# Rank scatter of 128 row tiles: 15 in place of 12 tiles as row copies from HBM to HBM, and loads of one row a partition

## The chip, the cores and the metric

The kernel runs on one core of a Trainium2 chip. The metric is the device time of one execution in microseconds, median of three runs. A profile of one execution, taken by the hardware profiler, gives the durations used below.

## The reference

Each of 8 batches has 2048 scores and 2048 rows of 2560 f32 (10 KB a row). A row goes to the place that the rank of its score has in its batch:

```python
B, N, D = 8, 2048, 2560            # x: (B, N, D) f32, scores: (B, N) f32
order = np.argsort(scores, axis=1)
ranks = np.argsort(order, axis=1)
out[b_idx, ranks, :] = x
```

The 168 MB of x are read once and the 168 MB of the output written once. The only arithmetic is the counting that gives the ranks.

## The kernel before

A tile is 128 rows of one batch, so there are 16 tiles a batch and 128 in all. The table `GROUPS` joins tiles into groups: `(first row, tiles in the group m, batches whose group goes directly)`. With m = 2 a partition of a load holds two neighbouring rows of x (20 KB in one piece), and the two tiles of the group are the even and the odd rows of 256. A group and a batch that the table names as direct are in the list `DIRECT`; all others are in `BULK`. Both lists go batch by batch, and inside a batch by `ORDER`.

*Ranks.* TensorE transposes the scores into columns (`s_col`, L167) and, for each batch, spreads its 2048 scores over all partitions (L188); VectorE copies these to `s_all` (L234). For each tile VectorE counts the scores that are smaller, or equal and earlier (L257: one count for the columns from the group's first on, one for the columns before it, and one product with a triangular mask over the group's own columns for ties). It adds the counts (L283, L289) to `rank`. A bulk group's ranks are cast to integers (`rank_i`, L306). A direct group's ranks are transposed by TensorE (L299), and VectorE turns them into byte addresses in the output (`rows_i`, L219); it does so after the counts of the group that follows.

*Bulk tiles.* SP issues the first `NBUF` loads (L119) as its first work. POOL then goes through `BULK` in order: it waits until the scatters of group k - `LAG` have landed, issues the load of group k + `NBUF` - `LAG` into the buffer that came free (L119), waits for group k's load and ranks, and issues one indirect scatter a tile (L375), 128 rows of 10 KB each.

*Direct tiles.* After its loads SP goes through `DIRECT`, and ACT, which has no other work, does the same. Each copies half of the rows of a tile. A loop (`Fori`, L331) makes four passes a tile; a pass loads 16 byte addresses from `rows_i` into registers (L332) and issues 16 copies of one row, from x to the output in HBM (L343), each split over the 16 DMA engines as 640 bytes a piece. Of the 12 direct tiles each of the two engines so copies 768 rows, in 48 passes. SP waits at the end for all rows and all scatters.

POOL's transfers go through one DMA queue, SP's through a second and ACT's through a third; all three are served by the same 16 DMA engines, and each queue has a ring on every one of them.

The lines that set the split, the buffers and the lead:

```python
GROUPS = [(0, 2, (0, 1, 2, 3, 4, 5)), (256, 2, ()), (512, 2, ()), ...]
NBUF = 8
LAG = 2
G = 16
```

Of the kernel before, what the change touches and what calls it, by code (L numbers as in the profile page):

```python
# [40 lines left out]
def kernel(  # L41
# [11 lines left out]

    GROUPS = [(0, 2, (0, 1, 2, 3, 4, 5)), (256, 2, ()), (512, 2, ()), (768, 2, ()), (1024, 2, ()), (1280, 2, ()), (1536, 2, ()), (1792, 2, ())]
    ORDER = [0, 1, 2, 3, 4, 5, 6, 7]
    MMAX = max(m for _, m, _ in GROUPS)
    MDIR = max([m for _, m, direct in GROUPS if direct], default=1)
    MBULK = max(m for _, m, direct in GROUPS if len(direct) < B)  # L60
    BULK = [(b, g) for b in range(B) for g in ORDER if b not in GROUPS[g][2]]
    DIRECT = [(b, g) for b in range(B) for g in ORDER if b in GROUPS[g][2]]

    PARTS = [(0, 128)]
    NBUF = 8
    LAG = 2
    G = 16

    def first_col(g):
        return GROUPS[g][0] // P  # L70

# [14 lines left out]
    rows_i = [pool.tile([MDIR, P], I32, name=f"rows_i{i}") for i in range(len(DIRECT))]  # L86
    xb = [pool.tile([P, MBULK * D], F32, name=f"x{i}") for i in range(NBUF)]
    ps_col = psum.tile([P, 512], F32, name="ps_col")
# [11 lines left out]
    with tc.tile_critical(no_gpsimd_drain=True):  # L100
# [5 lines left out]
        s_scores = nc.alloc_semaphore("scores")  # L106
        s_first = [nc.alloc_semaphore(f"first{i}") for i in range(NBUF)]
        s_load = [nc.alloc_semaphore(f"load{i}") for i in range(NBUF)]
        s_scat = [
            [nc.alloc_semaphore(f"scat{i}_{j}") for j in range(MBULK * len(PARTS))]  # L110
            for i in range(NBUF)
        ]
        s_rows = {sp: nc.alloc_semaphore("rows_sp"), act: nc.alloc_semaphore("rows_act")}
        n_scat = [[0] * (MBULK * len(PARTS)) for _ in range(NBUF)]

        def load(line, k, sem):
            b, g = BULK[k]
            r, m, _ = GROUPS[g]
            line.eng.dma_start(  # L119
                out=xb[k % NBUF][:, :m * D],  # L120
                in_=x[b, r:r + P * m, :].rearrange("(p j) d -> p (j d)", j=m),
            ).then_inc(sem, 16)
# [106 lines left out]
        for b in range(B):  # L229
# [11 lines left out]
            dve.after(dve, t_copied)  # L241
            for g in ORDER:
                r, m, _ = GROUPS[g]
# [110 lines left out]
        def scatters_done(k):  # L354
            i = k % NBUF
            for j in range(GROUPS[BULK[k][1]][1] * len(PARTS)):
                pl.wait(s_scat[i][j], 16 * n_scat[i][j])

        for k, (b, g) in enumerate(BULK):
            i = k % NBUF  # L360
            r, m, _ = GROUPS[g]
            if k >= LAG and k + NBUF - LAG < len(BULK):
                scatters_done(k - LAG)
                load(pl, k + NBUF - LAG, s_load[(k - LAG) % NBUF])
            if k < NBUF:
# [52 lines left out]
```

## Time and profile before

| | |
|---|---|
| median of 3 runs | 819.38 us (818.96 to 819.45) |
| time of the profiled execution | 818.96 us |
| its span | 817.2 us |
| VectorE busy | 408.7 us (50%), done by about 425 us |
| POOL busy | 142.2 us (17%) |
| HBM read and written | 167.84 MB and 167.77 MB, 411 GB/s over the span |
| first loads on SP | 8 of 2560 KB |
| loads on POOL | 50 of 2560 KB |
| scatters on POOL | 116 |
| row copies | 768 on SP, 768 on ACT |

The span runs from the first to the last instruction; the time of the execution holds a little more around it. Issuing a DMA does not count as busy time of an engine, so SP and ACT have next to no busy time though their row loops run for most of the span. They are read from the timeline, where the engine is written SPq or ACTq. The busy share of the DMA is the mean over 16 DMA engines.

### The profile page before, as it was taken

Reading aid. Unit: us, or ns where it says so; the run is one execution under the profiler, and the core shown is the slowest. Engines: PE = TensorE matmul, PEld = TensorE weight load, DVE = VectorE, ACT = ScalarE, POOL = GpSimd, SP = SyncE. Lnnn points to the kernel's source line nnn. Section 1 sums busy time; section 2 is a strip of 40 time slices with the busy share of each in tenths; the row PEclk is TensorE's granted clock in tenths of the full one; section 3 lists DMA queues with packets and bytes.
Section 4 is the critical chain, followed back from the end, with each engine's and each line's share of the span. In section 5 each row is a group of like instructions: output and inputs, shape, how many; then the busy total and the mean of one; then the engine's idle time right before and its main releaser. Section 6 shows DMA issues by size and latency. Waiting matters only on the chain.

```text
span 817.2 us, 8185 instructions
## 1 busy us (share of the span) xinstructions
PE 31.5 (4%) x150; PEld 27.1 (3%) x150; DVE 408.7 (50%) x962; ACT 0.0 (0%) x1; POOL 142.2 (17%) x175
## 2 busy tenths in 40 slices
PE   3001010010100101000000000000000000000000
PEld 3001010010100101000000000000000000000000
DVE  6999999999999999999960000000000000000000
ACT  0000000000000000000000000000000000000000
POOL 0111212121212111212111111212121212150000
PEclk9555555555555555555555555555555555555555
DMA  8999999999999999999999999999999999999810
GB/s 366 417 427 426 412 426 413 425 417 419 424 417 423 410 410 376 412 420 417 415 415 406 419 417 421 410 413 415 394 407 405 410 409 423 395 414 422 361 35 8
DMA packets 74248, 320.20 MB, mean 392 GB/s; under 512 B 27368, under 2 KB 51944, under 8 KB 51944
## 3 DMA queue, kind: packets, MB, share of 16 engines
q0 software_dynamic: 23904, 283.13, 82.6%
q1 hardware_dynamic: 25744, 28.95, 10.2%
q10 hardware_dynamic: 24576, 7.91, 4.0%
q14 instruction: 23, 0.19, 0.1%
q8 instruction: 1, 0.02, 0.0%
HBM read 167.84 MB, written 167.77 MB: 411 GB/s over the span
## 4 chain that ended last, share of the span: by engine, by line
DMA 44%; DVE 40%; POOL 3%; issue 3%; PE 1%; POOLq 0%; SPq 0%
DMA out_dram<-x,rank_i 42%; DVE trash L257 35%; DMA x<-in_x_dram 2%; POOL out_dram L375 2%; DVE s_all L234 2%; DVE rank L283 1%; DVE rank L289 1%; POOL x L119 1%; DVE rank_i L306 1%; PE ps_all L188 0%; DMA s_in<-in_scores_dram 0%; PE ps_col L167 0%; DVE rows_i L219 0%; POOLq L28 0%; DVE s_col L175 0%
## 5 line engine op out<-in xcount | busy, mean ns | idle before, releaser
L257 DVE TENSOR_SCALAR_CACHE_REDUCE trash<-s_all,s_col 128x1792 bf16<-128x1792 f32 (+7 forms) x240 | 314.5, 1345 | 0.3
L375 POOL DMA_INDIRECT out_dram<-x,rank_i x116 | 112.2, 967 | 65.4 <-issue 36.7
L119 POOL DMA_DIRECT2D x<-in_x_dram x50 | 28.2, 564 | 531.2 <-DMA out_dram<-x,rank_i 353.1
L257 DVE SCALAR_TENSOR_TENSOR trash<-s_all,s_col,mask 128x256 bf16<-128x256 f32 x128 | 61.4, 480 | 0.0
L188 PE MATMUL ps_all<-ident,s_col 128*128 128x128 f32 x128 | 27.5, 404 | 275.0 <-DVE s_all L234 274.6
L188 PEld LDWEIGHTS ps_all<-ident,s_col 128*128 128x128 f32 x128 | 24.6, 215 | 276.9 <-DVE s_all L234 276.5
L234 DVE COPY s_all<-ps_all 128x512 f32<-128x512 f32 x32 | 20.2, 685 | 1.9 <-PE ps_all L188 1.6
L257 DVE DVE_READ_ACCUMULATOR trash<-s_all,s_col 128x1 f32 x240 | 19.7, 82 | 0.0
L289 DVE TENSOR_TENSOR rank<-rank,acc 128x2 f32<-128x2 f32 x64 | 10.3, 161 | 2.2
L283 DVE TENSOR_TENSOR rank<-acc,acc 128x2 f32<-128x2 f32 x64 | 10.3, 161 | 2.2
L306 DVE CAST rank_i<-rank 128x2 int32<-128x2 f32 x58 | 9.7, 167 | 1.8
L257 DVE DVE_READ_ACCUMULATOR trash<-s_all,s_col,mask 128x1 f32 x128 | 10.5, 82 | 0.0
L175 DVE COPY s_col<-ps_col 128x128 f32<-128x128 f32 x1 | 0.3, 293 | 4.7 <-PE ps_col L167 4.7
L299 PE MATMUL ps_row<-ident,rank 128*2 128x128 f32 x6 | 1.9, 322 | 15.0 <-DVE rank L289 15.0
L167 PE MATMUL ps_col<-ident,s_in 8*128 8x8 f32 x16 | 2.1, 264 | 3.8 <-DMA s_in<-in_scores_dram 3.8
L167 PEld LDWEIGHTS ps_col<-ident,s_in 8*128 8x128 f32 x16 | 2.0, 211 | 3.8 <-DMA s_in<-in_scores_dram 3.8
L219 DVE TENSOR_SCALAR rows_i<-ps_row 2x128 int32<-2x128 f32 x6 | 1.6, 272 | 0.0
L299 PEld LDWEIGHTS ps_row<-ident,rank 128*2 128x2 f32 x6 | 0.5, 80 | 17.1 <-DVE rank L289 17.1
L148 POOL TENSOR_SCALAR_AFFINE_SELECT mask<-mask 128x256 f32<-128x256 f32 x2 | 0.8, 398 | 0.0
L160 DVE MEMSET acc<- 128x128 f32 x1 | 0.2, 165 | 1.1 <-SPq L100 1.1
L131 POOL MEMSET mask<- 128x512 f32 x1 | 0.5, 525 | 0.0
L130 POOL MEMSET ident<- 128x128 f32 x1 | 0.2, 204 | 0.5 <-SPq L100 0.5
(6 smaller groups left out, 0.7 us busy)
## 6 DMA issues: line engine op xcount, KB each, us to landing
x<-in_x_dram POOLq DMA_DIRECT2D x50, 2560.0 KB, 19.3
x<-in_x_dram SPq DMA_DIRECT2D x8, 2560.0 KB, 31.4
out_dram<-in_x_dram ACTq DMA_DIRECT2D x768, 10.0 KB
out_dram<-in_x_dram SPq DMA_DIRECT2D x768, 10.0 KB
out_dram<-x,rank_i POOLq DMA_INDIRECT x116, 24.1
s_in<-in_scores_dram SPq DMA_DIRECT2D x1, 64.0 KB
```

Of the source, the lines that this page charges most:

```text
L119: line.eng.dma_start(out=xb[k % NBUF][:, :m * D], in_=x[b, r:r + P * m, :].rearrange("(p j) d -> p (j d)", j=m),).then_inc(sem, 16)
L148: nc.gpsimd.affine_select(out=part, in_=part, pattern=[[0, MMAX], [-1, P]], compare_op=OP.is_ge, fill=0.0, base=-half, channel_multiplier=1,)
L167: nc.tensor.transpose(out=ps_col[:, B * c:B * (c + 1)], in_=s_in[:, r + j:r + m * P:m], identity=ident[:B, :B],)
L188: nc.tensor.transpose(out=ps_all[:, P * c:P * (c + 1)], in_=s_col[:, c, b:b + 1].to_broadcast([P, P]), identity=ident[:],)
L219: nc.vector.tensor_scalar(out=rows_i[DIRECT.index((b, g))][:m, :], in0=ps_row[:m, :P], scalar1=float(b * N), scalar2=float(ROW), op0=OP.ad ...
L234: nc.vector.tensor_copy(out=s_all[:, 512 * q:512 * (q + 1)], in_=ps_all[:, 512 * q:512 * (q + 1)],)
L257: how.pop("do")(out=trash[i][:, :P * (hi_c - lo_c)], in0=s_all[:, P * lo_c:P * hi_c], accum_out=acc[which][:, col:col + 1], **how,)
L283: nc.vector.tensor_tensor(out=rank[:, cols], in0=acc[0][:, cols], in1=acc[1][:, cols], op=OP.add)
L289: nc.vector.tensor_tensor(out=rank[:, cols], in0=rank[:, cols], in1=acc[2][:, cols], op=OP.add)
L299: nc.tensor.transpose(out=ps_row[:m, :P], in_=rank[:, cols], identity=ident[:])
L306: nc.vector.tensor_copy(out=rank_i[:, cols], in_=rank[:, cols])
L375: nc.gpsimd.indirect_dma_start(out=out_flat, out_offset=bass.IndirectOffsetOnAxis(ap=(rank_t if lo else rank_i)[:hi - lo, col:col + 1], axis=0
```

## The change

```diff
-    GROUPS = [(0, 2, (0, 1, 2, 3, 4, 5)), (256, 2, ()), (512, 2, ()), (768, 2, ()), (1024, 2, ()), (1280, 2, ()), (1536, 2, ()), (1792, 2, ())]
-    ORDER = [0, 1, 2, 3, 4, 5, 6, 7]
+    GROUPS = [(0, 1, (0, 1, 2, 3, 4, 5, 6, 7)), (128, 1, (0, 1, 2, 3, 4, 5, 6)), (256, 1, ()), (384, 1, ()), (512, 1, ()), (640, 1, ()), (768, 1, ()), (896, 1, ()), (1024, 1, ()), (1152, 1, ()), (1280, 1, ()), (1408, 1, ()), (1536, 1, ()), (1664, 1, ()), (1792, 1, ()), (1920, 1, ())]
+    ORDER = [0, 1, 2, 3, 4, 5, 6, 7, 8, 9, 10, 11, 12, 13, 14, 15]
...
-    NBUF = 8
-    LAG = 2
+    NBUF = 15
+    LAG = 4
```

Every group is now one tile of 128 neighbouring rows. The first tile of all eight batches and the second tile of seven go directly: 15 tiles, 960 rows for each of SP and ACT. The other 113 tiles are loaded one by one, 1.31 MB each with one 10 KB row a partition, 15 of them by SP and 98 by POOL. There are 15 buffers of one tile in place of 8 of two, and POOL loads 11 tiles ahead of the one it scatters, where it was 6 pairs. The columns of the counts, the masks, the adds and the casts follow the group's size.

## The prediction

> **What bounds the kernel now.** I read the DMA part of the page first, then the stretches of the span, then the timelines of SP and ACT.
>
> ```profile
> DMA  8999999999999999999999999999999999999810
> ...
> q0 software_dynamic: 23904, 283.13, 82.6%
> q1 hardware_dynamic: 25744, 28.95, 10.2%
> q10 hardware_dynamic: 24576, 7.91, 4.0%
> ```
>
> The 16 DMA engines are full for 37 of 40 slices and nearly idle in the last two. q0 is POOL's queue (scatters and later loads), q1 is SP's, q10 ACT's. The stretches give the edge:
>
> ```profile
> 66.00:720.00 654.00, 20.13 (x87) 16.76 (x85) 351.09 (x832) 0.00 (x0) 121.56 (x147) 0.51 1.02 413
> 720.00:770.00 50.00, 0.00 (x0) 0.00 (x0) 0.00 (x0) 0.00 (x0) 12.32 (x13) 0.50 1.02 418
> 770.00:817.00 47.00, 0.00 (x0) 0.00 (x0) 0.00 (x0) 0.00 (x0) 0.00 (x0) 0.50 0.18 51
> ```
>
> The last three numbers of a line are clock, DMA share (over 1 where packets of one engine overlap) and GB/s. Until 770 us the DMA is the limit; after it the share is 0.18, and something else holds the end for 47 us. SP's timeline says what:
>
> ```profile
> 24.43 783.95 SPq L343 DMA_DIRECT2D out_dram<-in_x_dram  x768
> 80.15 624.72 SPq L343 DMA_DIRECT2D out_dram<-in_x_dram  x624
> 724.79 42.38 SPq L343 DMA_DIRECT2D out_dram<-in_x_dram  x32
> 783.38 11.68 SPq L343 DMA_DIRECT2D out_dram<-in_x_dram  x16
> 796.70 11.68 SPq L343 DMA_DIRECT2D out_dram<-in_x_dram  x16
> 24.39 53.83 ACTq L343 DMA_DIRECT2D out_dram<-in_x_dram  x64
> ```
>
> The row loops run through the whole span, and SP's last row leaves at 808.4. So the kernel ends with SP's loop, not with the scatters. (The chain of waits shows scatters and VectorE because a loop that is never idle has no wait to follow; its VectorE pieces up to 334 us are an artefact, as VectorE is then on batch 6 and POOL on about tile 50.) Three paces of a row follow. **Free**, the last two passes of 16 rows start 13.32 us apart: 0.833 us a row. **DMA full but the loop's own queue not backed up**, ACT's first 64 rows, the next pass starting at 79.8: 55.4/64 = 0.866. **Steady**, SP from 80.15 to the pass at 706.58: 626.4/624 = 1.004. A fourth, while only scatters run (724.79 to the pass at 769.98): 45.2/32 = 1.41.
>
> ```profile
> L343 SPq DMA_DIRECT2D out_dram<-in_x_dram x768: 520/529/2122, 24.4 to 807.9; - x192
> L332 SPq TENSOR_LOAD <-rows_i x48: 973/1641/3729, 23.0 to 795.5; - x48
> ```
>
> Minimum, median and maximum: an issue costs at least 520 ns, an address load at least 973 ns a pass. In the free stretch row issues start 0.741 us apart; 16 of these and about 1.46 us for load and loop make the 13.32. What is above that is blocking: a row sent too early finds the queue full (counted from issues and packets, at most about 32 rows of a queue are outstanding).
>
> **The change, part by part.**
>
> *Rows.* 12 tiles become 15, so each loop does 960 rows in place of 768, in 60 passes in place of 48. Instructions per row are unchanged. Even with no blocking ever, 960 x 0.833 = 800 us of sequencer time. This is the largest term.
>
> *Where the loops start.* The first rank is now of one column. The first count ended at 13.1, the second column's needs 3 us more, so rows_i comes near 17 instead of 22.5, and rows could start near 19 instead of 24.4. SP cannot use it: its first loads (15 of 1.31 MB, 19.7 MB, in place of 21.0) stand ahead of its rows in q1. Before, the last packet of these loads started at 65.7. In the trace a 20 KB load packet takes 761 ns (median), a 10 KB scatter packet 385, a row's share on one engine 34 + 9 (640 bytes and its semaphore). Queues alternate packet by packet, so q1 with 20 KB packets had two thirds of the rate beside q0; with 10 KB packets it has half. By 26 us (first scatter) q1 has moved (26 - 2)/0.39 = 61 of its 120 packets per engine; the other 59 at 0.39 + 0.385 + 0.04 = 0.82 us end at 74 to 76. By then SP has issued what its queue holds, about 35 rows.
>
> *Pace in the bulk.* This is the unknown. Between two packets of q0 an engine takes one of SP and one of ACT (after 770, on the engine that is still scattering, every 10 KB packet is followed by one of each), and a row is two packets, so two rounds. Before, a pair of tiles was 8 load rounds of 0.76 + 0.043 and 16 scatter rounds of 0.385 + 0.043, 13.3 us for 24 rounds or 12 rows: 1.11 us a row, measured 1.004. With 10 KB loads every round is 0.43: 0.86 a row, or 0.92 on an engine at 415 ns a packet as the last one ran. By that the queue now keeps up with the issue, whose pace under a full DMA is 0.866. Bounds: 0.833 (free) and 1.41 (the scatter stretch, where every q0 packet is 10 KB too; I take it for a property of scatters alone, as the loads' half of the time still writes no HBM). I take 0.89, midway between 0.866 and 0.92, because both limits are near; 0.866 to 1.004 go into the range.
>
> *Bulk.* Per engine, before until 770: 464 x 0.786 + 928 x 0.386 + some 1450 rows x 0.043 = 785 us of packets in 768 us. After: 904 x (0.392 + 0.386) + some 1600 x 0.043 = 772, so 755 us by the same ratio; with the slower start I take 762 for the end of the bulk. If 10 KB loads cost 0.41 instead, it is 16 us later; the loops are then slower for 16 us longer, worth 16 x (1 - 0.833/0.89) = 1 us at the end.
>
> *Edits at nothing.* VectorE: L283 and L289 64 more each (161 ns), 55 more casts (167), 9 more rows_i (272), 8 more counts, against narrower mask products (480 ns at 256 wide): at most +35 us on 409. It is done near 425 us and the last scatter issues at 738; without that cover it would delay scatters one for one. PE: 9 more transposes of 0.3 us, beside it. POOL: 48 more load issues of 0.56 + 0.30 us; a tile needs 2.1 us of POOL in 6.7 us, and POOL sat 531 us idle before L119. If POOL were full, scatters would trail by 41 us. Buffers: 11 tiles ahead, four scattered, against six pairs and two; the queue is never empty in either (share 1.02). End: 7 more semaphore waits on SP at 0.07 us.
>
> *The sum.* 35 rows by 76; to 724 at 0.89, 728 more; to 762 at 1.41 (the same scatter-only end), 27; so 170 remain, x 0.833 = 142, loop over at 904. Before, the same count gives 770 + 48 x 0.833 = 810 against a span of 817.2: 7.2 us after it, now 7.7. The profiled run's time is 1.8 above its span (818.96), the median 0.4 above that run. 904 + 9.9 = **914**.
>
> The Trainium skill ("DMA: Bandwidth & Descriptors", section "Issuing engines are not separate DMA queues") holds that issue time is usually small beside the transfer. Here the row is 520 ns of issue against 43 ns on each engine, so the measurement decides; by the page's rule the loops would not matter and the kernel would end with the bulk, about 772. The same page's "Rules for kernel authors" speaks against the change: it calls transfers under 64 KB mostly overhead, and each row copy is 10 KB.
>
> **The rivals.**
>
> *B: the pace stays at 1.004.* For: one engine's backlog sets blocking, and why that engine lags is not shown. 648/1.004 = 645, 707 by 762, 253 x 0.833 = 211: 973 + 10 = 983.
>
> *C: the all-10 KB stream behaves like the scatter stretch, 1.41 throughout.* 460, 522, 438 x 0.833 = 365: 1127 + 10 = 1137. Against: ACT's first passes ran beside scatters at 0.866.
>
> *D: not slower.* The loops never block, start at 19 and run under the free pace. Place: the passes on SP. Price: 60 passes of 13.0 give 19 + 780 + 10 = 809; it decides from 13.15 us a pass down (19 + 789 + 10 = 818). Against: none of the 47 intervals on either queue was under 13.3, and 13.32 gives 828.
>
> *That the change does less than it says:* if the 32-row cap on SP were gone and the end stretch ran at 0.866, (762 - 19)/0.866 = 858 rows, 102 x 0.833 = 85: 857. This is the low edge of my own case.
>
> **How the numbers follow.** My case 0.72 (857 at best, 0.92 a row gives 933), B 0.18, C 0.06, D 0.04. The range runs from 857 to 980, close to B. Under 0.2% (1.6 us) a measurement of this kernel cannot tell from no change; D splits into faster 0.03 and same 0.01, the rest is slower, 0.96.
>
> **What would show it.** Right: SP's L343 group x960 ends near 900, and the DMA share falls to about 0.2 from 762 on for over 100 us; SP's passes in the middle last 14.0 to 14.7 us. B shows passes of 16, C of 22. Wrong: passes under 13.2 us, a bulk that lasts beyond 800, gaps in the DMA share before 700, or SP's loop ending before ACT's.

## The result and the profile after

The changed kernel takes 927.95 us (median of 4 runs, 925.32 to 931.61), against 819.17 for the kernel before in the same comparison: ratio 1.137, 95% interval 1.126 to 1.148. It is slower, 14 us above the predicted 914 and inside the range. The profiled execution took 925.32 us, its span is 923.6. Executions of one kernel differ more than the 0.2% that the prediction allowed: the kernel before took 807.56 to 819.45 us in this comparison and 808 to 834 over those below, so a difference under 2% is not read as a gain here.

The page of the changed kernel, DMA share and GB/s in 40 slices of 23.1 us, and the queues:

```profile
DMA  9999999999999999999999999999999995111110
GB/s 373 410 426 417 415 416 416 415 417 419 417 419 415 418 417 418 419 417 405 396 398 383 382 393 393 388 398 390 390 383 392 394 421 197 29 24 24 25 19 10
...
q0 software_dynamic: 30384, 276.58, 72.7%
q1 hardware_dynamic: 32896, 29.62, 9.8%
q10 hardware_dynamic: 30720, 9.89, 4.6%
```

Before, two slices at the end were nearly empty; now it is six. The stretches of the changed kernel (the last three numbers are clock, DMA share, GB/s):

```profile
76.00:716.00 640.00, 20.97 (x91) 17.40 (x91) 355.24 (x993) 0.00 (x0) 139.67 (x182) 0.51 1.02 405
716.00:771.00 55.00, 0.00 (x0) 0.00 (x0) 0.00 (x0) 0.00 (x0) 13.53 (x15) 0.50 1.01 406
771.00:923.00 152.00, 0.00 (x0) 0.00 (x0) 0.00 (x0) 0.00 (x0) 0.00 (x0) 0.50 0.13 26
```

For most DMA engines the bulk ends where it ended before (771 against 770 us); the last packets of POOL's queue ended at 788.9 and 785.8. Nearly all that was lost lies behind it: 152 us at a DMA share of 0.13, in place of 47 at 0.18. The timelines of SP and ACT say who works there:

```profile
21.36 49.69 SPq L343 DMA_DIRECT2D out_dram<-in_x_dram  x32
89.31 624.96 SPq L343 DMA_DIRECT2D out_dram<-in_x_dram  x688
716.26 53.25 SPq L343 DMA_DIRECT2D out_dram<-in_x_dram  x48
771.13 133.10 SPq L343 DMA_DIRECT2D out_dram<-in_x_dram  x160
21.36 896.13 SPq L343 DMA_DIRECT2D out_dram<-in_x_dram  x960
18.38 869.82 ACTq L343 DMA_DIRECT2D out_dram<-in_x_dram  x960
```

SP's loop ends at 917.5 and the program 6 us later. The paces by the starts of the passes: (716.26 - 89.31)/688 = 0.911 us a row in the bulk, where it was 1.004; (771.13 - 716.26)/48 = 1.14 in the scatter-only end, where it was 1.41; and 0.842 when the DMA engines are free (the next pass after these 160 rows starts at 905.8). The rows did get faster in the bulk, but there are 192 more of them in each loop.

```profile
L343 SPq DMA_DIRECT2D out_dram<-in_x_dram x960: 361/521/6546, 21.4 to 917.0; - x192
L332 SPq TENSOR_LOAD <-rows_i x60: 974/1135/2944, 19.9 to 904.6; - x60
```

An issue and an address load still cost what they cost at best (the median issue takes 521 ns, the shortest address load 974). What has shrunk is the waiting: the median address load was 1641 ns and is 1135.

### The profile page after: what moved, and what is told of

The parts are those of the page before. It is cut to its first block, busy times and chain, and to the rows that moved or that the text cites. A ratio compares the mean times of both kernels' runs of the same rounds, so it can differ in the third digit from the quotient of the medians.

```text
span 923.6 us, 10105 instructions
## 1 busy us (share of the span) xinstructions
PE 33.0 (4%) x159; PEld 27.7 (3%) x159; DVE 422.1 (46%) x1170; ACT 0.0 (0%) x1; POOL 166.3 (18%) x220
## 4 chain that ended last, share of the span: by engine, by line
DVE 44%; issue 26%; POOL 7%; DMA 3%; PE 1%; POOLq 0%; SPq 0%
DVE trash L257 36%; POOL out_dram L375 5%; POOL x L119 3%; DMA x<-in_x_dram 3%; DVE rank L283 2%; DVE rank L289 2%; DVE s_all L234 2%; DVE rank_i L306 2%; PE ps_all L188 0%; DVE rows_i L219 0%; DMA s_in<-in_scores_dram 0%; PE ps_col L167 0%; POOLq L28 0%; DVE s_col L175 0%; SPq L413 0%
## 5 line engine op out<-in xcount | busy, mean ns | idle before, releaser
L257 DVE TENSOR_SCALAR_CACHE_REDUCE trash<-s_all,s_col 128x256 bf16<-128x256 f32 (+15 forms) x248 | 315.0, 1305 | 0.3
L119 POOL DMA_DIRECT2D x<-in_x_dram x98 | 55.2, 564 | 510.5 <-DMA out_dram<-x,rank_i 355.1
L375 POOL DMA_INDIRECT out_dram<-x,rank_i x113 | 109.6, 970 | 71.6 <-issue 36.7
L257 DVE SCALAR_TENSOR_TENSOR trash<-s_all,s_col,mask 128x128 bf16<-128x128 f32 x128 | 44.3, 346 | 0.0
L283 DVE TENSOR_TENSOR rank<-acc,acc 128x1 f32<-128x1 f32 x128 | 20.5, 160 | 4.4
L289 DVE TENSOR_TENSOR rank<-rank,acc 128x1 f32<-128x1 f32 x128 | 20.4, 159 | 4.4
L306 DVE CAST rank_i<-rank 128x1 int32<-128x1 f32 x113 | 17.2, 152 | 3.7
L299 PE MATMUL ps_row<-ident,rank 128*1 128x128 f32 x15 | 4.8, 322 | 69.8 <-DVE rank L289 51.9
L219 DVE TENSOR_SCALAR rows_i<-ps_row 1x128 int32<-1x128 f32 x15 | 4.1, 272 | 0.0
```

The lines of the kernel that those rows point to most:

```text
L119: line.eng.dma_start(out=xb[k % NBUF][:, :m * D], in_=x[b, r:r + P * m, :].rearrange("(p j) d -> p (j d)", j=m),).then_inc(sem, 16)
L219: nc.vector.tensor_scalar(out=rows_i[DIRECT.index((b, g))][:m, :], in0=ps_row[:m, :P], scalar1=float(b * N), scalar2=float(ROW), op0=OP.ad ...
L257: how.pop("do")(out=trash[i][:, :P * (hi_c - lo_c)], in0=s_all[:, P * lo_c:P * hi_c], accum_out=acc[which][:, col:col + 1], **how,)
L283: nc.vector.tensor_tensor(out=rank[:, cols], in0=acc[0][:, cols], in1=acc[1][:, cols], op=OP.add)
L289: nc.vector.tensor_tensor(out=rank[:, cols], in0=rank[:, cols], in1=acc[2][:, cols], op=OP.add)
L299: nc.tensor.transpose(out=ps_row[:m, :P], in_=rank[:, cols], identity=ident[:])
```

## The experiments

The theory: each loop needs its sequencer for some 0.84 us a row whatever the DMA engines do, so 960 rows end behind the bulk. Against it stood that loads of one row a partition cost the time, that the busy DMA engines hold the rows back, and that packet size has nothing to do with it. The runs fall into three comparisons on three different chips, in which the kernel before took 820, 830 and 823 us (medians); each ratio is against the kernel before in its own comparison.

### 12 direct tiles, loads of one row a partition

```diff
-(128, 1, (0, 1, 2, 3, 4, 5, 6))
+(128, 1, (0, 1, 2, 3))
```

> The changed kernel with 12 direct tiles in place of 15 (all eight first tiles and four second ones); loads still one row a partition, 15 buffers, lag 4. Theory (the number of rows a loop sets the end): 768 rows a loop, 35 issued by 76 us, the other 733 at 0.911 us, so the loops end near 745 to 760, before the bulk; the bulk then sets the end: 3 more tiles of 16 packets of 0.39 us an engine are 19 us on the 772 (most engines) and 789 us (last engine) of the changed kernel, so a time of 795 to 820. Rival (loads of one row a partition cost the time): 890 or more.

810.33 us, ratio 0.9936 (0.9885 to 0.9988). Timeline of SP, then the stretches after its end:

```profile
21.18 723.99 SPq L343 DMA_DIRECT2D out_dram<-in_x_dram  x768
```
```profile
745.00:788.00 43.00, 0.00 (x0) 0.00 (x0) 0.00 (x0) 0.00 (x0) 11.85 (x13) 0.50 1.01 425
788.00:808.00 20.00, 0.00 (x0) 0.00 (x0) 0.00 (x0) 0.00 (x0) 0.00 (x0) 0.50 0.10 44
```

The loops are through at 745, the DMA stays full to 788, and the bulk's last engine ends at 802.7. With three tiles fewer the same loads are no loss. Nor are they a gain that could be told from none: two of thirteen executions of the kernel before took 808 and 809 us in the same comparison. So the loss of the change is in the three tiles.

### 15 direct tiles, loads of two rows a partition

```diff
-GROUPS = [(0, 2, (0, 1, 2, 3, 4, 5)), (256, 2, ()), ...
+GROUPS = [(0, 1, (0, 1, 2, 3, 4, 5, 6, 7)), (128, 1, (0, 1, 2, 3, 4, 5, 6)), (256, 2, ()), ...
```

> The kernel before with the same 15 direct tiles as the changed one (as groups of one tile), and the other groups still loaded two rows a partition, 8 buffers, lag 2. Theory (rows set the end, and small load packets let the queue keep up): pace 1.00 us a row as in the kernel before: 35 rows by 66 us, 634 more by 703, 35 in the scatter-only end up to 753, the last 256 at 0.84: loop ends near 969, time 965 to 990, slower than the changed kernel by some 45 us. Rival A (loads of one row a partition cost the time): 800 to 830. Rival B (packet size does not matter for the pace): 915 to 930.

One second tile that stays in the bulk (batch 7) is loaded alone, with one row a partition. 959.32 us, ratio 1.177 (1.162 to 1.192), a little under the expected 965 to 990. The profiled execution took 973.5, the longest of five (the others 958.9 to 961.9). Timeline of SP:

```profile
80.36 621.67 SPq L343 DMA_DIRECT2D out_dram<-in_x_dram  x624
18.63 944.77 SPq L343 DMA_DIRECT2D out_dram<-in_x_dram  x960
```

The next pass starts at 703.7, so a row takes 623.3/624 = 0.999 us, as in the kernel before. If all the 14 us by which this execution was longer lay in these 624 rows, the others would still have had 0.977. The two halves of the change are now apart: three more direct tiles cost about 140 us (959 against 820; with loads of one row a partition 118, 928 against 810), and the rest of the change gives some 31 back (928 against 959; the intervals of the two ratios do not meet). The faster pace of the rows, 0.911 against 0.999, has the sign and at least the size for it. Rival A has the wrong sign. Rival B, that the pace stays the same, falls too, though packet size is not shown as the only reason: 15 buffers in place of 8 and a lag of 4 in place of 2 come with the 10 KB packets, and no run parts them.

### The rows alone

```diff
-for k in range(NBUF):
+for k in range(0):
...
-for k, (b, g) in enumerate(BULK):
+for k, (b, g) in enumerate(BULK[:0]):
```

> The changed kernel without any load or scatter of the 113 bulk tiles (they are left out); ranks and the 960 rows of each loop as they are. Theory (the sequencers' own issue time is most of it): 60 passes of 13.3 us from 19 us on, loop ends near 818, time 815 to 840 with the DMA engines nearly idle. Rival (the rows wait for DMA engines that are busy with the bulk): without the bulk the loops end far earlier, below 650 us.

830.38 us, one execution. Its timeline of SP and the stretch of its whole span (no ACT work but row issues):

```profile
18.38 807.48 SPq L343 DMA_DIRECT2D out_dram<-in_x_dram  x960
```
```profile
2.00:828.00 826.00, 35.29 (x159) 29.39 (x159) 421.85 (x1169) 0.00 (x0) 0.27 (x2) 0.52 0.15 24
```

This is the plainest line of the study: with nothing else on the DMA engines, 15 tiles of row copies take longer than the whole kernel before (820 in the same comparison). The share is 0.15 and, counted from issues and packets, never more than two rows of SP were waiting for their packets to start; the time is the sequencers', 0.842 us a row. All the bulk adds to the changed kernel is about 98 us of starting late and waiting.

### The first loads on POOL, 15 tiles

```diff
-for k in range(NBUF):
+for k in range(0):
     load(sp, k, s_first[k])
...
+for k in range(NBUF): load(pl, k, s_first[k])
```

> The changed kernel with the first 15 loads issued by POOL in place of SP, so that SP's queue holds rows only. Theory (SP's rows stand behind its loads until 76 us): SP runs as ACT did, whose loop ended 29 us earlier (last issue 887.7 against 917.0): time 893 to 905. Rival (the first loads do not matter, SP is slower for another reason): 920 to 930.

894.28 us, the median of four executions: three from 894.25 to 896.68, which fit the expectation, and one of 875.49, for which no run shows a reason. All four lie 28 us or more below every execution of the changed kernel. SP's timeline, from the profiled one (894.25):

```profile
18.40 868.07 SPq L344 DMA_DIRECT2D out_dram<-in_x_dram  x960
```

SP ends at 886.5, close to where ACT had ended (888.2) in the changed kernel. So in this execution the rows that stood behind SP's own loads until 76 us were worth the 30 us expected of them (917.5 to 886.5).

### 32 addresses a pass, 15 tiles

```diff
-G = 16
+G = 32
```

> The changed kernel with 32 addresses a pass in place of 16, so 30 passes a loop in place of 60; row copies and DMA traffic are the same. Theory (a loop runs at its sequencer's pace: 0.741 us a row and about 1.46 us a pass for address load and loop, more under traffic): each pass saved is worth 1.46 to 2 us, so the loop ends 44 to 55 us earlier at most, less what the queue then holds back: time 875 to 895. Rival (the queue's service by the DMA engines sets the pace): no difference, 915 to 930.

929.02 us, ratio 1.118 (1.113 to 1.123). The changed kernel had 927.95 and 1.137 in its own comparison: the time is the same, and the lower ratio comes of a kernel before that was slower in this comparison (830). The group of address loads on SP:

```profile
L332 SPq TENSOR_LOAD <-rows_i x30: 1875/3048/4875, 20.0 to 895.2; - x30
```

Half as many loads take twice as long at the least (1875 ns for 32 addresses, 974 for 16): 56 ns for each of the 16 added addresses, which leaves some 70 ns that are paid once a pass. My expectation took 1.46 us as a price of a pass; most of it is a price of 16 rows. So this run does not tell the two theories apart, and its rival's number came out for another reason.

### Fewer or freer rows on the kernel before

Four runs ask whether the end of the kernel before was the loops too. First 11 direct tiles (eight first tiles and three second ones) with loads of two rows a partition; the five second tiles that stay in the bulk are loaded alone, with one row a partition:

```diff
-GROUPS = [(0, 2, (0, 1, 2, 3, 4, 5)), (256, 2, ()), ...
+GROUPS = [(0, 1, (0, 1, 2, 3, 4, 5, 6, 7)), (128, 1, (0, 1, 2)), (256, 2, ()), ...
```

> The kernel before with 11 direct tiles in place of 12 (eight first tiles and three second ones), the rest loaded two rows a partition. Theory (rows set the end of the kernel before too): 64 rows fewer a loop at the free and slow paces of its end, so the loops end before the bulk, whose last engine ended at 786 in the kernel before, under 2 us later with one more tile: time 794 to 806, faster than the kernel before by 2%. Rival (the bulk is the limit and each tile taken out of it is a gain): 820 to 828.

797.08 us, ratio 0.960 (0.956 to 0.964). SP's timeline and the last stretches:

```profile
18.42 708.15 SPq L343 DMA_DIRECT2D out_dram<-in_x_dram  x704
```
```profile
700.00:784.00 84.00, 0.00 (x0) 0.00 (x0) 0.00 (x0) 0.00 (x0) 17.93 (x20) 0.50 1.00 408
784.00:795.00 11.00, 0.00 (x0) 0.00 (x0) 0.00 (x0) 0.00 (x0) 0.00 (x0) 0.50 0.05 22
```

SP's loop issues its last row at 726, the DMA is full to 784, the bulk's last engine ends at 790.6 and the program 5 us later. With one tile *fewer* of row copies the DMA is the bound to the end. (Groups of one tile also let the rows start at 18.4 in place of 24.4, which is small beside the 82 us by which SP's loop ends earlier.)

The same gain by the other way, 12 tiles and the first 8 loads on POOL:

```diff
-for k in range(NBUF):
+for k in range(0):
     load(sp, k, s_first[k])
...
+for k in range(NBUF): load(pl, k, s_first[k])
```

> The kernel before with its first 8 loads issued by POOL in place of SP; 12 direct tiles, 16 addresses a pass. Theory: SP's loop runs as ACT's did (last issue 793.2 against 807.9), so it ends 12 to 15 us earlier: time 802 to 810. Rival: 818 to 824.

800.13 us, ratio 0.964 (0.960 to 0.968), a gain of 30 where 12 to 15 were expected. SP's timeline:

```profile
24.19 751.21 SPq L344 DMA_DIRECT2D out_dram<-in_x_dram  x768
```

Both loops have issued their last rows by 775.4 and the bulk's last engine ends at 788.7, so the bulk is the end here. Two things stay open: why the kernel before took 830 in this comparison, as it was not profiled there, and why ACT's loop, which the edit leaves alone, ended 20 us earlier (773.4) than in the profile of the kernel before (793.8).

With 32 addresses a pass on top:

```diff
-G = 16
+G = 32
```

> The kernel before with its first 8 loads on POOL and 32 addresses a pass; 12 direct tiles. Theory: both loops end some 30 us earlier than in the kernel before, near 775, before the bulk's last engine (786): the bulk sets the end, 793 to 803. Rival (queue service sets the pace of the loops under 20 KB loads, so fewer address loads give nothing): the loops end as in the run with the first loads on POOL alone, within 3 us of it.

802.97 us, ratio 0.967 (0.963 to 0.971). SP's timeline:

```profile
25.16 761.51 SPq L344 DMA_DIRECT2D out_dram<-in_x_dram  x768
```

The time is in the expected band, but not for its reason: the loops ended at 786.7, 11 us later than with 16 addresses, so neither the theory (775) nor the rival (within 3 us) had it. The bulk's last engine ended at 791.3.

Both edits that help, 11 tiles and loads on POOL:

```diff
-GROUPS = [(0, 2, (0, 1, 2, 3, 4, 5)), (256, 2, ()), ...
+GROUPS = [(0, 1, (0, 1, 2, 3, 4, 5, 6, 7)), (128, 1, (0, 1, 2)), (256, 2, ()), ...
...
-for k in range(NBUF):
+for k in range(0):
     load(sp, k, s_first[k])
...
+for k in range(NBUF): load(pl, k, s_first[k])
```

> Both edits at once on the kernel before: 11 direct tiles and the first loads on POOL, loads two rows a partition. Theory (once the loops end before the bulk, the bulk is the end, and loops that end still earlier give nothing): 794 to 804, as each of the two alone. Rival (the two gains add): 770 to 785.

798.88 us, ratio 0.972 (0.968 to 0.977). SP's timeline:

```profile
18.61 674.03 SPq L344 DMA_DIRECT2D out_dram<-in_x_dram  x704
```

The loops end at 693 and nothing is gained by it: the gains do not add.

### The bulk alone

```diff
-for b, g in DIRECT:
+for b, g in DIRECT[:0]:
```

> The kernel before without its 12 direct tiles (the row copies are left out); 116 bulk tiles as they are. Theory (a direct tile takes as much of the DMA engines as its packets say, 128 x 0.043 = 5.5 us an engine against 6.2 us for a bulk tile): the bulk ends about 65 us earlier, most engines near 711 and the last near 725, time 725 to 745. Rival (row copies use gaps that the bulk leaves): the bulk ends as in the kernel before, 786, time 790 to 800.

745.26 us, at the upper edge of the expected band. The packets carry no engine's number, but their rate falls at 726 to 730, so most DMA engines ended there; the last packet ended at 735.8. The stretch up to the fall:

```profile
2.00:720.00 718.00, 32.66 (x150) 28.39 (x150) 408.65 (x961) 141.02 (x169) 0.52 1.01 419
```

Against 773 and 785.8 in the kernel before (819 in its profile), the row copies of 12 tiles cost the DMA engines some 46 us, 3.8 a tile, where their packet times added up to 5.5. A bulk tile costs (728 - 2)/116 = 6.3. So the rows are neither free nor as dear as I had them: a tile moved from bulk to rows relieves the DMA by 2.5 us and puts 64 x 0.84 = 54 us on each loop. This is one execution, and the step from 5.5 to 3.8 is not explained, but for a small part: 80 of the 1536 rows, 3.4 us of packets, were issued only after 768 us, when the bulk was all but over.

## Why the prediction was right, point by point

*What bounds the kernel.* Right: SP's loop and not the scatters. With eleven tiles the kernel before gains 4% (797 against 830 in that comparison, 3% against the 819 to 823 of the others), and its end is then the bulk.

*Rows.* Right, and the largest term. I had 960 x 0.833 = 800 us; the rows alone took 807.5, from their start at 18.4.

*Where the loops start.* Right: the last packet of SP's loads started at 76.2 (74 to 76 foretold), 32 rows were issued by 73.8, and SP with its loads on POOL ends 31 us earlier.

*Pace in the bulk.* The direction was right and its size a little off, and this makes up the 14 us: 0.911, not 0.89. Over the 640 us from 76 to 716 this is 640/0.89 - 640/0.911 = 17 rows, at 0.842 us each 14 us. From 89 to 716 the mean issue on SP was 0.562 us (0.526 when the DMA is free) and the mean address load 1.46 (0.98): 0.036 + 0.48/16 = 0.066 above the free 0.842. In the kernel before it was 0.633 and 1.82. So the excess of the issues fell to a third (0.036 of 0.107), while address loads under a full DMA kept more than half of theirs (0.48 of 0.84), and I had put none of it above ACT's early 0.866. The packets bear out that the queue was less backed up: in the mean of the same stretch, rows of SP that were issued and whose packets had not started numbered 18 in the kernel before and 8 in the changed one. The round-robin count itself was rough: it gave 1.11 for the kernel before, which measured 1.004.

*The scatter-only end.* Two misses that cancel, by luck. I took the pace of before, 1.41, to 762; it was 1.14 to 771. By my sum 801 rows would have been out at 771, with 18 of them too many from the bulk; 784 were. Nor was 1.41 a property of the scatters alone, as I had taken it: with 15 tiles and 20 KB load packets the like passes ran at 1.39 (703.7 to 748.35 us), with 10 KB ones at 1.14.

*Bulk.* 9 us too early. A 10 KB packet of q0 took 397 ns in the mean, not 389. From 76 to 420 us it was 387 and q0 moved as before; after that 407 to 414 in stretches of 100 us, and the rate fell from some 417 GB/s to between 382 and 398 (the GB/s line above). What slows them is open. As foretold, it mattered little for the end.

*Edits at nothing.* VectorE has 422.1 us (+13, at most +35 foretold), POOL 166.3 (+24); both are done long before the end.

*The rivals.* B's premise, an unchanged pace, is refuted by 0.911 against 0.999 at equal rows. C is refuted by the same line. D would have needed passes under 13.15 us; even alone they took 13.5 (16 x 0.842).

*The Trainium skill.* "DMA: Bandwidth & Descriptors", section "Issuing engines are not separate DMA queues", has issue time as usually small beside the transfer. For the use of the engines the rows alone show the opposite: 0.84 us of sequencer a row with the DMA engines at a share of 0.15, so the loops set the end and not the bulk.

## What to carry to other kernels

When many small DMAs come from a loop, price the loop first by itself: its copies times the issue pace read from a stretch in which the DMA is idle. Here 960 x 0.84 us was more than the bulk took, and no relief of the DMA could pay for it. A loop that issues through the whole span shows no wait in the chain; look at the timeline of its engine and at who is still at work when the DMA share falls. The split between two paths is right when both end together, and beyond that point a gain on the path that is not last is worth nothing (797, 800 and 799 us for either edit and for both).

## What the runs showed of the hardware that I had not expected

- An address load into registers costs by the address: 974 ns for 16, 1875 for 32, at the least.
- With 20 KB loads row packets fall behind, by their number those of one DMA engine. In the kernel with 11 tiles SP's last row was issued at 726.0 and its last packet started at 760.8, with about 30 packets over 10 us late, what one engine would hold of some 30 rows. With 10 KB loads (12 tiles) the last packet came 4.6 us after the last issue (744.6 and 749.2). That this engine's backlog is what blocks the issues fits, but no run took it away alone.
- Load packets grow slower in the later part of a run. In the kernel before the 20 KB loads took 763 ns from 66 to 240 us and 800 from 420 to 720, while its 10 KB scatters stayed at 386 to 387. With loads of one row a partition, where loads and scatters have the same size, the mean went from 387 (76 to 420 us) to 410 and 411 (from 420 to the end of SP's bulk), with 15 and with 12 direct tiles. No run explains it.
